# A two-layer hybrid decoder trunk on one Trainium2 core: FFN, norms, gate stages, indexer, attention and output moved from the compiler framework's order into the kernel's own list scheduler

## The chip, the core and the metric

The kernel runs on one core of one Trainium2 chip. A core has five engines, each with an instruction queue of its own that is worked off in the order in which the program has it: PE (TensorE, matrix products and transposes by product with the identity, results in PSUM), DVE (VectorE), ACT (ScalarE), POOL (GpSimd) and SP (SyncE, which here only issues DMAs). The engines wait for each other through semaphores. The metric is the device time of one execution in microseconds; the kernel before has a median of 2846.68 us in 3 runs (2844.36 to 2846.99).

## What is computed

One sequence of 256 tokens, 2048 wide, in f32, through two layers. Cut to what matters:

```python
for i in range(2):
    h = gdn_mixer(x, ...) if i == 0 else dsa_mixer(x, ...)
    x = layer_norm(ALPHA * x + h, ln1_g[i], ln1_b[i])
    f = (silu(causal_conv3(x @ w_gate[i])) * (x @ w_up[i])) @ w_down[i]   # 2048 -> 5120 -> 2048
    x = layer_norm(ALPHA * x + f, ln2_g[i], ln2_b[i])
    x = x + sigmoid(x @ ple_w_gate[i]) * (p[i] @ ple_w_proj[i])
```

`gdn_mixer` is gated DeltaNet linear attention: a projection to 12,352 columns, a causal convolution over four tokens on q, k and v, 32 value heads, the delta rule in chunks, an output norm gated by silu(z) and a projection from 4096 back to 2048. `dsa_mixer` is sparse attention: a projection to 5264 columns (2048 q, 512 k, 512 v, 2048 for 16 indexer heads, 128 indexer keys and 16 weights), a layer norm on the indexer keys, a score for each pair of tokens (ReLU products summed over the heads), the 64 best keys of each token, a softmax over those with a bias by distance, and a projection from 2048 to 2048.

## The kernel before

**Products.** An f32 number is held as two halves, hi (rounded to the type that PE multiplies at full rate) and lo (the rest), and a product is hi·hi + lo·hi + hi·lo. Weights come from HBM in blocks of 128x1024 f32 (512 KB; 1024 columns of SBUF are four k-tiles of 256 columns or two of 512): SP issues the load into one of three `raw` buffers, ACT makes hi (`hi`, L205), DVE makes lo (`lo`, L206), three buffers each, and PE works the block off. There are two forms. `gemm_t_steps` (L211) has the weights as the stationary operand and gives transposed results, `mm_ps`, two PSUM tiles of 128 columns of weights each: per k-tile two products of 512 columns with hi (L224: both halves of x at once) and two of 256 with lo (L228). `gemm_steps` (L236) has x stationary, `b_ps`, two tiles for the two halves of 128 tokens: per k-tile and half L248, L249 (x hi and x lo with the weights' hi) and L252 (with their lo). PSUM has four `mm` tiles, two `sp` and two `bk`. `xT` is x transposed in hi and lo, `x` the residual stream, two tiles of 128 tokens.

**Two ways of ordering.** The DeltaNet part (`gdn_plan`, L413 on) is already placed by the kernel's own list scheduler, `Plan` (L70 to L158). Every piece of work is a task with an engine, an estimated cost, the tasks that it follows, the buffers that it takes and gives, and a rank. `Plan.run` keeps a clock for each engine, and again and again takes the task that can start first, at equal start the one of lowest rank, and emits its instructions; the order in which an engine's tasks are emitted is the order of its queue. The choice is one line (`s` is the estimated start, `at` the engine's clock):

```python
key = (s if s > at + 0.05 else 0.0, rank, t.order)
```

 `place` in it makes five tasks of a weight block: the load (SP, 0.38 us, landing 2.2 us of bus time and 1.8 us later), the cast (ACT 1.06 us, or DVE 0.8), the subtraction (DVE 1.23) and two product tasks (`product(0)` with hi, `product(1)` with lo). The cast and the subtraction have rank 0 when the block is the next one on PE, and 3 otherwise. Everything behind it is written as ordinary code in program order, `project`, `layer_norm`, `ffn`, `prepare`, `ple`, `distances` and `dsa` (L354 to L403 and L1164 to L1410), which the framework schedules with hand-set priorities: weight casts are moved ahead by 1000 places (`W_AHEAD`), the norm is given high priority, and a few orders are forced one by one (`after`).

**What follows the DeltaNet part.** `project` (L1164) multiplies a matrix in five column blocks, adds it to the residual (L324, L326) with its statistics (L328), and then calls `layer_norm`:

```python
blocks = ((0, 512), (512, 512), (1024, 512), (1536, 256), (1792, 256))
```

Before the norm it puts two columns of `ple_w_proj` (`fill`, L1246, into `pw`) on PE as work that doesn't depend on it. `layer_norm` (L354) gets 1/sqrt by an integer guess and three Newton steps (`rsqrt`, L338 to L352), scales tokens 0 to 127 on DVE (L372) and the others on ACT (L373), transposes on PE (`n_ps`, L383), evicts with gain and bias on ACT (`xb`, L389), and makes hi and lo of `xT` on DVE (L392, L393). `affine` (L395) later applies gain (`lng`) and bias (`lnb`) to x itself on DVE (L399, L400), a quarter of the columns at a time, from rows that POOL loads into one buffer each. `ffn` (L1186): 20 column pairs, gate then up, each 256 columns; the convolution and silu of gate and the product with up on ACT and DVE into `hT`; then `project` with `ffn_w_down`, 40 k-tiles. `ple` (L1256): four columns of `ple_w_gate`, the first two side by side, then sigmoid (L1264), times `pw` (L1265), plus x (L1266) and, in layer 0, the transposes of the next x (`t_ps`, L295, with L288 and L289), in layer 1 the store (L1268). `dsa` (L1307): the columns of indexer keys (144 wide) beside the first two indexer heads; the key norm reads its sums out of PSUM (L1319 to L1324); the indexer heads with their small products (L1338); eight loads of the distance bias by POOL (`bias<-fx`, L1356); the 64 best by eight rounds of maximum and replacement; 32 additions of the mask on POOL; keys, values, and then `attend` for each head.

## Time and profile before

| | |
|---|---|
| median of 3 runs | 2846.68 us |
| the profiled execution | 2843.02 us |
| its span, first to last instruction | 2841.2 us |
| weights and other data moved | 519.70 MB, mean 183 GB/s |
| DeltaNet part, to the first norm | about 0 to 893 us |
| FFN of layer 0, to its second norm | about 900 to 1577 us |
| gate stage of layer 0 | about 1580 to 1681 us |
| sparse attention and its projection | about 1677 to 2060 us |
| FFN of layer 1 | about 2065 to 2740 us |
| gate stage of layer 1 and end | about 2742 to 2841 us |

How to read the lines. A row of a group has source line, engine, operation, what it writes <- reads, shape and count, then its busy time and the mean of one, then the idle time of that engine ahead of it and what ended it. In a row of the timeline the first number is the start in us from the span's start, the second the time from the first start to the last end, `x8` a run of eight, and in brackets the engine's idle time ahead of it and what ended that. Matmuls are pipelined, so their busy times overlap; what one costs in a stream is the step from start to start. In a row of a stretch stand its length, then each engine's busy time and instruction count, the granted share of PE's clock, the DMA engines' busy share and GB/s.

### The profile page before, as it was taken

What the parts mean: (1) busy time and instruction counts of PE and PEld (TensorE: products, weight loads), DVE (VectorE), ACT (ScalarE), POOL (GpSimd) and SP (SyncE); (2) the same over time, 40 slices, a digit from 0 to 9 for tenths busy, and PEclk for the clock granted to TensorE, in tenths of its full rate; (3) what the DMA queues carried; (4) which work ended last, traced back from release to release, by engine and by line L of the source; (5) the groups of instructions that cost most, each with busy time, mean ns of one, the idle gap of its engine ahead of it and who ended that gap; (6) DMA issues with size and microseconds to landing.
All of it is one profiled execution on the core that took longest, in us unless ns stands there. A gap on an engine that the chain in (4) does not pass through costs nothing. (4 is left out here: it accounts for less than half of the span.)

```text
span 2841.2 us, 40908 instructions
## 1 busy us (share of the span) xinstructions
PE 2806.2 (99%) x15654; PEld 2436.4 (86%) x15654; DVE 1900.9 (67%) x2995; ACT 1397.7 (49%) x2244; POOL 114.6 (4%) x191
## 2 busy tenths in 40 slices
PE   8999999999999999999999999999999999999998
PEld 7888888888888888888889788888888888888887
DVE  6887778877778666666544755765676666655465
ACT  4745555553435555555433544455465555543353
POOL 0100001000000000000000000400000000000000
PEclk9999999999999999999999999999999999999999
DMA  6765656555545666666555565544556666655555
GB/s 191 222 184 160 184 151 185 172 153 169 154 134 174 188 202 205 205 202 200 192 193 187 190 197 170 177 147 151 177 183 195 196 190 194 197 191 193 190 188 182
DMA packets 415077, 519.70 MB, mean 183 GB/s; under 512 B 19708, under 2 KB 313984, under 8 KB 414880
## 3 DMA queue, kind: packets, MB, share of 16 engines
q1 hardware_dynamic: 407136, 496.76, 56.6%
q0 software_dynamic: 7744, 20.32, 3.0%
q8 instruction: 123, 2.02, 0.3%
q14 instruction: 74, 0.61, 0.1%
HBM read 512.76 MB, written 7.39 MB: 183 GB/s over the span
## 5 line engine op out<-in xcount | busy, mean ns | idle before, releaser
L206 DVE TENSOR_TENSOR lo<-raw,hi 128x1024 fp32r<-128x1024 f32 (+1 forms) x676 | 827.2, 1225 | 625.5 <-ACT hi L205 616.2
L205 ACT ACTIVATE hi<-raw 128x1024 fp32r<-128x1024 f32 (+1 forms) x676 | 714.1, 1057 | 931.5 <-PE b_ps L249 404.2
L224 PE MATMUL mm_ps<-xT,hi 128*128 128x512 f32 x3136 | 792.1, 394 | 2.8 <-DVE rs L345 1.6
L224 PEld LDWEIGHTS mm_ps<-xT,hi 128*128 128x128 f32 x3136 | 565.1, 189 | 103.6 <-issue 2.6
L228 PEld LDWEIGHTS mm_ps<-xT,lo 128*128 128x128 f32 x3136 | 431.0, 191 | 30.4
L228 PE MATMUL mm_ps<-xT,lo 128*128 128x256 f32 x3136 | 447.4, 284 | 0.0
L539 DVE TENSOR_TENSOR lo<-raw,hi 128x1024 fp32r<-128x1024 f32 x249 | 304.0, 1221 | 48.3 <-ACT hi L531 26.0
L531 ACT ACTIVATE hi<-raw 128x1024 fp32r<-128x1024 f32 x183 | 193.3, 1057 | 192.6 <-PE b_ps L506 84.4
L498 PE MATMUL mm_ps<-xT,hi 128*128 128x512 f32 (+1 forms) x1040 | 264.1, 396 | 4.4 <-ACT hi L531 2.7
L498 PEld LDWEIGHTS mm_ps<-xT,hi 128*128 128x128 f32 (+1 forms) x1040 | 189.5, 189 | 42.9 <-ACT hi L531 3.1
L248 PE MATMUL b_ps<-hi,hTA 128*128 128x512 f32 (+1 forms) x640 | 212.6, 347 | 0.0
L249 PE MATMUL b_ps<-hi,hTA 128*128 128x512 f32 (+1 forms) x640 | 212.4, 347 | 0.0
L248 PE MATMUL b_ps<-hi,xT 128*128 128x512 f32 (+2 forms) x480 | 173.3, 370 | 1.6 <-ACT sg L1264 1.6
L249 PE MATMUL b_ps<-hi,xT 128*128 128x512 f32 (+2 forms) x480 | 173.7, 371 | 0.0
L495 PE MATMUL mm_ps<-xT,lo 128*128 128x256 f32 (+1 forms) x1040 | 149.6, 287 | 0.0
L495 PEld LDWEIGHTS mm_ps<-xT,lo 128*128 128x128 f32 (+1 forms) x1040 | 137.1, 189 | 5.8
L252 PE MATMUL b_ps<-lo,hTA 128*128 128x512 f32 (+1 forms) x640 | 138.6, 347 | 0.0
L248 PEld LDWEIGHTS b_ps<-hi,hTA 128*128 128x128 f32 x640 | 121.3, 190 | 15.0
L249 PEld LDWEIGHTS b_ps<-hi,hTA 128*128 128x128 f32 x640 | 121.4, 190 | 14.9
L252 PE MATMUL b_ps<-lo,xT 128*128 128x512 f32 (+2 forms) x480 | 118.5, 370 | 2.8 <-DVE lo L206 2.8
L252 PEld LDWEIGHTS b_ps<-lo,hTA 128*128 128x128 f32 x640 | 105.2, 190 | 15.0
L248 PEld LDWEIGHTS b_ps<-hi,xT 128*128 128x128 f32 x480 | 90.6, 189 | 17.6 <-ACT sg L1264 2.9
(300 smaller groups left out, 3352.8 us busy)
## 6 DMA issues: line engine op xcount, KB each, us to landing
raw<-in_gdn_w_in SPq DMA_DIRECT2D x193, 512.0 KB, 4.0
raw<-in_ffn_w_gate SPq DMA_DIRECT2D x160, 512.0 KB, 3.9
raw<-in_ffn_w_up SPq DMA_DIRECT2D x160, 512.0 KB, 3.7
raw<-in_ffn_w_down SPq DMA_DIRECT2D x160, 512.0 KB, 3.6
raw<-in_dsa_w_in SPq DMA_DIRECT2D x80, 512.0 KB, 3.6
raw<-in_gdn_w_o SPq DMA_DIRECT2D x64, 512.0 KB, 3.7
raw<-in_ple_w_gate SPq DMA_DIRECT2D x64, 512.0 KB, 3.9
raw<-in_dsa_w_o SPq DMA_DIRECT2D x32, 512.0 KB, 3.9
```

What stands on the lines that cost most here:

```text
L205: nc.scalar.activation(hi, raw, AF.Copy)
L206: ins = nc.vector.tensor_tensor(lo, raw, hi.bitcast(F32), op=ALU.subtract)
L224: nc.tensor.matmul(q[:m, :], hi[:, k, o:o + m], x[:, k0 + k].rearrange("p a b -> p (a b)"), start=k0 + k == 0, stop=False)
L228: nc.tensor.matmul(q[:m, S:], lo[:, k, o:o + m], x[:, k0 + k, 0, :], start=False, stop=k0 + k == kt - 1)
L248: nc.tensor.matmul(ps[a][:, :n], xh, hi[:, k, :], start=k0 + k == 0, stop=False)
L249: nc.tensor.matmul(ps[a][:, :n], xl, hi[:, k, :], start=False, stop=False)
L252: self.last = nc.tensor.matmul(ps[a][:, :n], x(k0 + k)[:, 0, a * P:(a + 1) * P], lo[:, k, :], start=False, stop=k0 + k == kt - 1)
L495: nc.tensor.matmul(ps[o][:m, S:], lo[:, k, o * P:o * P + m], x(k0 + k)[:, 0], start=False, stop=e)
L498: nc.tensor.matmul(ps[o][:m], hi[:, k, o * P:o * P + m], x(k0 + k).rearrange("p a b -> p (a b)"), start=s, stop=False)
L531: nc.scalar.activation(hi, box["raw"], AF.Copy)
L539: nc.vector.tensor_tensor(lo, box["raw"], box["hi"].bitcast(F32), op=ALU.subtract)
```

## The change

`gdn`, `project`, `layer_norm`, `ffn`, `prepare`, `ple`, `distances`, `dsa` and their helpers are gone; the same computation is written as tasks of one `Plan` that covers the whole kernel, from the first load to the last store. In the plan:

- The three stages after DeltaNet open their SBUF areas by a POOL task without instructions (`stage`) that follows all tasks added before it; only what writes into the new area follows it.
- Weight blocks stay in one list, `order`; a block's load now follows the load of the block before (`behind`: emitted after it, without waiting for its end). A block that isn't the next one has rank 3.45 for its cast and subtraction instead of 3.
- `project` has four columns of 512 instead of three and two of 256. The last block of the fourth is cut by token half (`split`): all products of tokens 0 to 127, then those of 128 to 255, each with its own task, so that sum and statistics of the first half follow that half alone. `ple`'s last column is cut in the same way.
- The Newton iteration is one cubic step and one quadratic step instead of three quadratic ones: ten DVE instructions instead of twelve.
- `norm`: residual, statistics, root and scaling have ranks below zero; each eviction may go to ACT or to DVE, the rounding to DVE or to ACT, whichever is free first by the plan's clock; the fills' products, the transposes and the first FFN blocks are tasks of PE that start when their inputs are there by that clock. The first FFN block needs the first two pairs of k-tiles complete.
- `affine`: each load of gain or bias follows a given weight block (in FFN one quarter every 32 blocks; for the gate stage block 16 from the end of what is placed then), its use has rank 4.6, below almost everything.
- `dsa`: ACT copies the indexer keys' sums out of PSUM before the key norm; each bias load follows the product of a later weight block (every third one); small products are tasks with rank 1, ahead of the weight blocks' 5 and 4.
- In the DeltaNet part the tasks stay; some ranks change (table `RANK`), above all for taps, decays and table switches.

The core of the diff:

```diff
+    def add(self, engine, cost, emit, after=(), take=(), give=(), rank=5, lag=None, tail=0.0, bus=0.0, table=None,
+            other=None, behind=()):
...
+        for late, tasks in ((True, after), (False, behind)):
+            for d in tasks:
+                t.left += 1
+                d.then.append((t, late))
...
-            d = add(Q, 0.38, load, take=["raw"], rank=i, bus=2.2, tail=1.8)
-            h = add(A, 1.06, high, [d], take=["hi"], rank=urgent,
-                    other=(V, 0.8, cast, lambda: 3 if i <= plan.now + 1 else 9))
-            l = add(V, 1.23, low, [h], take=["lo"], give=["raw"], rank=urgent)
...
+            near = lambda: i <= plan.now + R["near"]
+            urgent = lambda: 0 if near() else R["later"]
...
+            d = b["load"] = add(Q, 0.38, load, take=["raw"], rank=i, bus=2.2 * size, tail=1.8,
+                                behind=[last["load"]] if i else ())
+            h = add(A, 0.2 + 0.86 * size, high, [d], take=["hi"], rank=urgent,
+                    other=(V, 0.1 + 0.6 * size, cast, lambda: R["cast"] if near() else 9))
+            l = add(V, 0.1 + 1.13 * size, low, [h], take=["lo"], give=["raw"], rank=urgent)
...
+            one, two = (2, 3) if b["halves"] else (0, 1)
...
-                nc.vector.tensor_scalar(zz, zz, -0.5, None, op0=ALU.mult)
...
+            def cubic():
+                y, u, zz = box["y"], box["t"], z()
                 nc.vector.tensor_tensor(u, y, y, op=ALU.mult)
                 nc.vector.tensor_tensor(u, u, zz, op=ALU.mult)
+                nc.vector.scalar_tensor_tensor(u, u, -1.25 / c, u, op0=ALU.add, op1=ALU.mult)
+                nc.vector.scalar_tensor_tensor(y, u, 1.875, y, op0=ALU.add, op1=ALU.mult)
...
-            for _ in range(3):
-                d = add(V, 0.55, step, [d], rank=rank)
+            d = add(V, 0.72, cubic, [d], rank=rank)
+            d = add(V, 0.55, step, [d], rank=rank)
...
+        def project(src, kt, x, ready, scale, opened):
...
+            for nb in range(4):
+                def done(state, task, nb=nb):
+                    for a in range(2):
+                        xs_ = self.x[:, a, nb * 512:(nb + 1) * 512]
+                        d = add(V, 0.69, lambda a=a, xs_=xs_: self.residual(xs_, state["ps"][a], scale),
+                                [task[a] if nb == 3 else task], give=["mm"], rank=-2 if nb == 3 else 1)
+                        stat[a].append(add(V, 0.69, lambda a=a, xs_=xs_: nc.vector.bn_stats(st()[:, a, nb], xs_),
+                                           [d, opened], rank=-2 if nb == 3 else 3))
+                r.append(column(src, 0, nb * 512, 512, kt, x, False, ready, done, split=nb == 3))
...
+            for k0 in range(0, KT, 2):
+                n = 2 if k0 < 4 else 0 if k0 % 4 else 4
+                rank = k0 / 8 - 1
...
+                x = add(E, 0.45, turn, before, take=[tag], rank=1, lag=0.25)
+                turned.append(x)
+                for k in range(2):
+                    x = add(A, 0.565, lambda k=k, f=put_a: f(k), [x, gbd], take=["xb"] * (not k), give=[tag] * k, rank=rank,
+                            other=(V, 0.42, lambda k=k, f=put_v: f(k), lambda rank=rank: rank + R["put"]))
...
+                d = add(G, 0.55, lambda r=r, src=src: nc.gpsimd.dma_start(
+                    out=r(), in_=bass.AP(tensor=src.tensor, offset=src.offset + nb * 512, ap=[[0, P], [1, 512]])),
+                    gate, take=[tag], bus=1.1, tail=3.0)
...
+                    c = add(A, 0.4, lambda a=a, kv=kv: nc.scalar.activation(kv(), state["ps"][a][:, :P + 16], AF.Copy),
+                            [task, opened], give=["mm"], rank=1)
...
+            loads = fetch([order[i0 + 3 * j]["task"] for j in range(8)])
...
+                run(c[3])
...
+                run(w["fill"](0))
+                run(w["fill"](1))
+                pairs, turned = norm(st, stat, gb1)
+                gate, up, down = ffn(w, pairs, ready)
+                run(two(gate(0), up(0)))
+                for n in range(2, D_FF // P, 2):
+                    run(gate(n))
+                    run(up(n))
```

More of the change, by code (lines that the diff above doesn't have):

```diff
@@ L153, in run @@
                 self.room[name].sort()
-            for n in t.then:
+            for n, late in t.then:
                 n.left -= 1
-                n.ready = max(n.ready, t.end + (n.lag if n.engine != t.engine or t.tail else 0.0))
+                if late:
+                    n.ready = max(n.ready, t.end + (n.lag if n.engine != t.engine or t.tail else 0.0))
                 if not n.left:
                     self.enter(n)
-        assert len(self.log) == self.count, (len(self.log), self.count)
+        assert len(self.log) == len(self.tasks), (len(self.log), len(self.tasks))
 class Trunk:
+    RANK = {'near': 1,
+            'later': 3.45,
+            'cast': 3,
+            'soon': 2.5,
+            'due': 2,
+            'tap': 4.5,
+            'rows': 3.5,
+            'solve0': 2.2,
+            'solve1': 3.7,
+            'weigh0': 1.5,
+            'weigh1': 5,
+            'dim': 3,
+            'calm': 1.5,
+            'wild': 4,
+            'swap': 2,
+            'put': 0,
+            'round': 2}
     def __init__(self, nc, tc, ctx, t):
-        self.nc, self.tc, self.t, self.heads = nc, tc, t, {}
+        self.nc, self.tc, self.t = nc, tc, t
         pool = lambda **k: ctx.enter_context(tc.tile_pool(**k))
@@ L321, in residual, with run @@
-    def residual(self, xb, ps, st, scale=ALPHA):
+    def run(self, out):
+        engines = {getattr(mybir.EngineType, e) for e in ("PE", "DVE", "Activation", "Pool", "SP")}
+        with self.tc.manual_schedule(engines=engines):
+            self.build(out)
+    def residual(self, xb, ps, scale):
         if scale == 1.0:
@@ L475, in gdn_plan, with column @@
         order = []
-        def column(src, rows, c0, n, kt, x, wide, ready, done):
+        def column(src, rows, c0, n, kt, x, wide, ready, done, nk=None, split=False):
             state = {}
-            nk = min(1024 // n, kt)
-            first = True
+            nk = nk or min(1024 // n, kt)
+            unit = 0.2274 if n == 512 else max(0.112, n / 2400 + 0.0133)
             out = []
@@ L805, in decays @@
         def decays(g, tile, take, out, back, after=()):
[L807 to L808 removed]
+            d = add(Q, 0.4, lambda: rows_into(g, tile()), [rows["go"], *after], take=[take], rank=lambda: plan.now + R["rows"], bus=2.2, tail=3.5)
+            calm = lambda: R["calm"] if plan.table == "exp" else R["wild"]
             def clamp(a, hs):
@@ new lines, in marked, with soon, folded, fold @@
+        def marked():
+            i = len(order) - 1
+            order[i]["bends"] = True
+            due = []
+            def soon():
+                if not due:
+                    due.append(next((j for j in range(i + 1, len(order)) if "bends" in order[j]), i + 99))
+                return R["soon"] if due[0] <= plan.now + R["due"] else R["tap"]
+            return soon
+        def folded(state, n, task, out, rank=1, take=(), more=()):
+            box = {}
+            def fold():
+                box["t"] = new("fold", [S], 2)
+                nc.scalar.activation(box["t"], state["ps"][n][:, S:], AF.Copy)
+            x = add(A, 0.37, fold, [task, *more], take=["fold"], rank=rank)
+            return add(V, 0.42, lambda: nc.vector.tensor_tensor(out(), state["ps"][n][:, :S], box["t"], op=ALU.add),
+                       [x], take=take, give=["mm", "fold"], rank=rank)
```

975 lines of the change are left out of this document (502 added, 473 removed).

## The prediction

> **What bounds the kernel now.** I read the page's busy times first, then who waits for whom on PE, then the timelines of the places named there.
>
> ```profile
> span 2841.2 us, 40908 instructions
> PE 2806.2 (99%) x15654; PEld 2436.4 (86%) x15654; DVE 1900.9 (67%) x2995; ACT 1397.7 (49%) x2244; POOL 114.6 (4%) x191
> L206 DVE TENSOR_TENSOR lo<-raw,hi 128x1024 fp32r<-128x1024 f32 (+1 forms) x676 | 827.2, 1225 | 625.5 <-ACT hi L205 616.2
> L205 ACT ACTIVATE hi<-raw 128x1024 fp32r<-128x1024 f32 (+1 forms) x676 | 714.1, 1057 | 931.5 <-PE b_ps L249 404.2
> ```
>
> PE is the bound; DVE and ACT have a third and a half of the span free. An order can therefore only win what PE loses by standing, and the casts of 676 weight blocks outside the DeltaNet part, which is planned already, are the work that could newly hold PE up. The list of PE's waits says how much stands:
>
> ```profile
> PE n_ps L383 <- ACT xb L389: 5.8, 8, 0.9
> PE b_ps L252 <- DVE lo L206: 2.8, 2, 1.4
> PE mm_ps L498 <- ACT hi L531: 2.7, 1, 2.7
> PE t_ps L295 <- DVE x L1266: 2.0, 2, 1.6
> PE mm_ps L224 <- DVE rs L345: 1.6, 1, 1.6
> PE b_ps L248 <- ACT sg L1264: 1.6, 3, 0.8
> PE mm_ps L224 <- ACT hi L205: 0.9, 1, 0.9
> ```
>
> The columns are the total, the times and the longest. L498 is the planned part; the other six rows, 14.7 us, stand at the norms (L383), in the gate stages (L252, L295, L248) and where the sparse attention begins (L224). So the ceiling of a mere reordering is about 15 us and what surrounds each stop. FFN gate, up and down have no row at all. A steady stretch there shows why: 575 matmuls, half of them 230 ns apart, half 120 ns, are 100.6 us in 100 us, while DVE is at 65%.
>
> ```profile
> 1100.00:1200.00 100.00, 100.00 (x575) 88.14 (x574) 65.02 (x95) 51.71 (x80) 2.31 (x5) 1.00 0.68 205
> 1098.13 2.00 PE L224 MATMUL mm_ps<-xT,hi 128*128 128x512 f32 x8
> 1099.97 1.12 PE L228 MATMUL mm_ps<-xT,lo 128*128 128x256 f32 x8
> 1100.92 2.00 PE L224 MATMUL mm_ps<-xT,hi 128*128 128x512 f32 x8
> ```
>
> (1098.13 to 1099.97 is 8 steps of 230 ns, to 1100.92 another 8 of 119; a block of 512 KB of weights lasts 2.79 us.)
>
> **The change part by part. Wider last columns.** Each projection ended in two columns 256 wide; now it is one of 512. Both kinds of block carry 512 KB; only their starts matter:
>
> ```profile
> 2704.68 0.28 PE L248 MATMUL b_ps<-hi,hTA 128*128 128x256 f32 x1
> 2707.56 0.28 PE L248 MATMUL b_ps<-hi,hTA 128*128 128x256 f32 x1
> 1605.48 0.39 PE L248 MATMUL b_ps<-hi,xT 128*128 128x512 f32 x1
> 1608.20 0.39 PE L248 MATMUL b_ps<-hi,xT 128*128 128x512 f32 x1
> ```
>
> 2.88 us a block against 2.72. With 4, 40, 16 and 40 k-tiles, four to a block and two columns, there are 50 such blocks: 50 x 0.16 = **8.0 us less**, pure PE work and the surest term.
>
> **Norms.** PE has 24 transposes to do between the last product of the fills and the first gate product:
>
> ```profile
> 893.56 0.65 PE L383 MATMUL n_ps<-ident,x 128*128 128x128 f32 x2
> 896.27 0.33 PE L383 MATMUL n_ps<-ident,x 128*128 128x128 f32 x1 [0.77 <-ACT xb L389]
> 900.36 0.78 PE L224 MATMUL mm_ps<-xT,hi 128*128 128x512 f32 x1
> 896.59 1.22 DVE L206 TENSOR_TENSOR lo<-raw,hi 128x1024 fp32r<-128x1024 f32 x1
> 898.66 1.22 DVE L206 TENSOR_TENSOR lo<-raw,hi 128x1024 fp32r<-128x1024 f32 x1
> 895.21 1.92 ACT L389 ACTIVATE xb<-n_ps,gb 128x256 f32<-128x256 f32 x4
> 892.24 0.16 DVE L351 SCALAR_TENSOR_TENSOR rs<-rt,rs 128x2 f32<-128x2 f32 x1
> ```
>
> Two weight casts of 1.22 us stand between the pieces of xT that PE waits for, and ACT alone evicts four halves in 1.92 us. In the plan the norm's tasks rank ahead of casts that aren't due, and an eviction may go to DVE. The inverse square root takes ten instructions instead of twelve (0.16 us each, row L351), and the statistics of the first 128 tokens run beside the last products of the other 128. Against that, the last sum and statistics are 512 wide, not 256: an estimate of 0.6 us more on the path, half of 0.65 us for each of the two, from the 512-wide DVE rows at the end of the kernel below. The row n_ps has 5.8 us for four norms; DVE must still do scale, round and subtract for two pairs before the first block, so I recover 4.0 of 5.8 (bounds 0 and 5.8).
>
> **Gate stages.**
>
> ```profile
> 1614.57 1.29 DVE L400 TENSOR_TENSOR x<-x,lnb 128x512 f32<-128x512 f32 x2 [3.35 <-DMA lnb<-in_ln_b]
> 1617.05 1.20 PE L252 MATMUL b_ps<-lo,xT 128*128 128x512 f32 x4 [1.44 <-DVE lo L206]
> 1628.06 1.28 ACT L1264 ACT_TABLE_LOAD   x1
> 1629.36 0.60 ACT L1264 ACTIVATE sg<-b_ps 128x512 f32<-128x512 f32 x1
> 1630.01 0.50 PE L248 MATMUL b_ps<-hi,xT 128*128 128x512 f32 x1 [0.85 <-ACT sg L1264]
> 1619.93 1.07 PE L252 MATMUL b_ps<-lo,xT 128*128 128x512 f32 x4
> lnb<-in_ln_b POOLq DMA_DIRECT2D x16, 256.0 KB, 5.8
> ```
>
> DVE waits in its order for the norm's gain and bias rows, the casts stand behind it, PE stands. The plan asks for these rows 16 blocks earlier and puts their use at a low rank; the transposes (the t_ps row, 1.6 at its longest) become tasks that PE takes when they are ready, while it runs the attention's first blocks. Of 2.8 + 2.0 + 1.6 = 6.4 us I recover 5.5 (bounds 3 and 6.4). What speaks against it: the plan reckons 0.55 + 3.0 us for such a load where the row shows 5.8, so DVE can still stand 2 us with casts behind it; three raw, hi and lo buffers, two blocks or 5.4 us, cover that, and without cover it would be 2 us at each of the 8 places.
> The third column needs the sums that the sigmoid frees; from the end of column one it has 2.72 us, and table load and two sigmoids are 1.28 + 1.2 = 2.5, just enough. The Trainium skill (ScalarE: Activation LUTs, What ACT_TABLE_LOAD costs) gives a switch 2.66 us with the drain; by that the column would stand some 1.2 us longer in each stage and the sum be about 2.5 us smaller. Here the sigmoid starts 20 ns after the 1.28 us load, so I keep the row.
>
> **Where sparse attention begins.**
>
> ```profile
> 1682.50 5.95 POOL L1356 DMA_DIRECT2D bias<-fx  x8
> 1690.00:1695.00 5.00, 5.00 (x40) 4.75 (x38) 0.76 (x1) 0.69 (x1) 0.00 (x0) 1.00 1.04 350
> 1705.05 0.70 PE L224 MATMUL mm_ps<-xT,hi 128*128 128x512 f32 x2 [1.58 <-DVE rs L345]
> 1708.15 1.91 PE L228 MATMUL mm_ps<-xT,lo 128*128 128x256 f32 x8
> ```
>
> Eight bias loads go out at once and fill the DMA engines (share 1.04), so weights come late (the 0.9 us row); after it PE waits 1.6 us for the sums that the key norm reads, and then runs at half rate: 1.91 us for the eight steps that took 1.12. The change gates each bias load on a later block, and ACT copies the keys out at once (two copies, each narrower than the 512-wide ACT row of 0.60 us above). The waits added are POOL's: behind each gated load stand only the next one and the mask additions, needed when the heads come. I recover 0.9 + 1.6 + 0.8 = 3.3 (bounds 1 and 3.7).
>
> **Restarts and end.** A stop costs more than its idle time: the four products at 1617.05 take 1.20 us instead of the 1.07 of the group at 1619.93; the six rows count 17 stops, and 15 fewer at 0.13 are 2.0 (bounds 0.5 and 2.5).
>
> ```profile
> 2834.92 1.09 ACT L1264 ACTIVATE sg<-b_ps 128x512 f32<-128x512 f32 x2 [7.78 <-PE b_ps L252]
> 2836.76 1.29 DVE L1266 TENSOR_TENSOR x<-x,sg 128x512 f32<-128x512 f32 x2
> ```
>
> At the end two halves go through sigmoid, product and sum together, 3.1 us. With the last block cut by halves the first is done under the second's products; one half needs 2.0: **1.0 less** (0.3 to 1.2).
>
> **What it costs.** FFN, which loses nothing, now depends on estimated times. In the planned part the one cast row is L498, 2.7 us, at the very start. I charge 2.5 us (bounds 0 and 9, the latter 13 ns for each of 676 blocks). The new ranks inside the DeltaNet part I put at 0 (2 either way): PE's rows there are mostly the start.
>
> **Sum.** 8.0 + 4.0 + 5.5 + 3.3 + 2.0 + 1.0 - 2.5 = **21.3 us**. The profiled execution took 2843.0 us, its span and 1.8 us around it; it would take 2821.7. The median of the runs is 2846.68, 3.7 us above that execution; the predicted median is 2846.7 - 21.3 = **2825.4**. Lower bounds alone give 8 + 0 + 3 + 1 + 0.5 + 0.3 - 9 = 3.8, or 2843; the upper ones with 2 us from DeltaNet 8 + 5.8 + 6.4 + 3.7 + 2.5 + 1.2 + 2 = 29.6, or 2817.
>
> **Rivals.** *Casts come late* (slower). The plan makes a cast urgent only when its block is next. Cast and subtraction are 1.06 + 1.23 = 2.3 us against a block's 2.79; half a microsecond of fold or tap ahead of them in a fixed order and PE stands. Its size is the 0.9 us of the L224 row; in one block of fifteen that is 676 / 15 x 0.9 = 41 us, against gains of 23.8: 2864. It decides from one block in 26 (35 ns a block). For it: three buffers only. Against it: DVE at 65% in the FFN, and a single such row in the planned part. 8%.
> *The stops only move* (no change; also the case in which the plan's clock is so far from the chip's that its order isn't what it takes it for). The named waits go, but equal ones arise at the same joints, since DVE is the limit there; only the wide columns and the end remain, less the FFN's charge at its worst: 8 + 1 - 9 + 2 = 2, up to 8: 2839 to 2845. For it: at the first norm DVE is busy 12.16 us of 12.58. 18%.
>
> ```profile
> 887.78:900.36 12.58, 10.64 (x52) 8.36 (x50) 12.16 (x34) 9.80 (x17) 0.00 (x0) 0.89 0.32 94
> ```
>
> *Half rate at every joint.* That row's clock, 0.89, shows a stretch at half rate after PE's idling. If all four norms and the gate stages met such a stretch, each would cost up to twice the 0.8 us seen above, some 5 us in all: 2830. The Trainium skill (TensorE: Matmul & The Clock Gate, the part on the HAM clock gate) halves the clock after one idle window of 3.4 us that runs freely; which joint is hit is then chance. The row agrees that it happens. 5%.
> *More than that*: the plan also fills the remaining stops; 2810 to 2815. 7%.
>
> **How the numbers follow.** The forecast, 2815 to 2837, has 62%. From 2813 to 2843 lies that, the clock case and most of the second rival: about 80%. Under 0.2% (5.7 us) this kernel's measurement can't tell a change from none. Faster than 2841.0: 62 + 5 + 7 and 8 of the second rival's 18, 82%; within it the other 10%; slower 8%.
>
> **What would show it.** Right: no L206-like row over 1 us among PE's waits, n_ps under 2 us, no 128x256 products in the projections, DMA share under 0.9 where attention begins, the last store about 1 us nearer to the last product. Wrong: PE rows on hi or lo spread over many times in FFN (first rival), or n_ps, t_ps and sg rows of the old size under new lines (second).

## The result and the profile after

The changed kernel takes **2816.85 us** (median of 4 runs, 2816.54 to 2818.76) against 2846.64 for the kernel before (4 runs beside it, 2844.36 to 2846.99): ratio 0.9898, 95% interval 0.9881 to 0.9916, 1.0% less time. The prediction had 2825.4 with a range of 2813 to 2843.

The profiled execution took 2816.92 us. It is 26.1 us shorter than the profiled execution of before, the medians differ by 29.8, since that execution of before lay 3.6 us under its median. Over all 42 runs of the kernel before in this document the median is 2843.3 us, and against that the gain is 26.4 us; some 3 us of the 29.8 belong to the four runs that happened to stand beside the changed kernel. The head of its page:

```profile
span 2815.1 us, 39629 instructions
PE 2789.1 (99%) x15054; PEld 2402.5 (85%) x15054; DVE 1889.9 (67%) x2932; ACT 1416.1 (50%) x2259; POOL 115.2 (4%) x191
```

PE has 600 matmuls fewer (the narrow columns' second halves) and stays the bound. Where the 26.1 us came from is read by cutting both traces at the same pieces of work (start to start of the first product of each kind):

| stretch | before, us | after, us | difference |
|---|---|---|---|
| start to first product | 5.28 | 5.13 | -0.2 |
| to the last product of the DeltaNet output | 882.50 | 882.23 | -0.3 |
| to the first down product, layer 0 (norm 1, FFN) | 461.75 | 459.93 | -1.8 |
| to norm 2 (down) | 226.86 | 224.70 | -2.2 |
| to the indexer keys (norm 2, gate stage) | 101.01 | 96.44 | -4.6 |
| to norm 3 (sparse attention and its projection) | 381.48 | 366.72 | **-14.8** |
| to the first down product, layer 1 (norm 3, FFN) | 453.37 | 455.09 | **+1.7** |
| to norm 4 (down) | 226.86 | 224.68 | -2.2 |
| to the last product (norm 4, gate stage) | 95.62 | 94.67 | -1.0 |
| end | 6.53 | 5.57 | -1.0 |

More than half of it is the sparse attention, to whose start the prediction gave 3.3 us. The stretch with norm 3, which was to gain, lost.

**Who waits for whom on PE, after.** Columns: the total, the times, the longest.

```profile
PE mm_ps L303 <- DVE xT L1116: 2.9, 2, 2.0
PE b_ps L310 <- DVE xT L1113: 2.6, 2, 1.3
PE n_ps L1089 <- ACT x L1081: 2.3, 5, 0.6
PE b_ps L310 <- DVE hi L345: 1.8, 2, 1.2
PE b_ps L311 <- DVE oT L934: 1.1, 1, 1.1
```

(The rows for `hi` and `oT` stand in the DeltaNet part; the list's other rows stand in the kernel's first 100 us or have 0.5 us at most.) The rows of the gate stages (lo, sg, t_ps) and of the start of the attention (rs) are gone. At the norms n_ps fell from 5.8 to 2.3, but 2.9 + 2.6 us of waits for `xT` are new: the stop moved from the transposes to the first product behind them.

**Norm 3 after**, timeline: start, time from first start to last end, engine, line, what it writes <- reads.

```profile
2034.20 3.49 DVE L349 TENSOR_TENSOR lo<-raw,hi 128x1024 fp32r<-128x1024 f32 x3
2034.41 1.06 ACT L341 ACTIVATE hi<-raw 128x1024 fp32r<-128x1024 f32 x1 [0.77 <-PE b_ps L311]
2035.38 1.08 ACT L1081 ACTIVATE x<-x,lnm,rs 128x256 f32<-128x256 f32 x2
2036.02 1.04 PE L1089 MATMUL n_ps<-ident,x 128*128 128x128 f32 x7 [0.60 <-ACT x L1081]
2036.36 0.58 ACT L1038 ACTIVATE pw<-b_ps 128x512 f32<-128x512 f32 x1
2036.84 1.91 ACT L1100 ACTIVATE xb<-n_ps,gb 128x256 f32<-128x256 f32 x4
2039.08 3.58 PE L303 MATMUL mm_ps<-xT,hi 128*128 128x512 f32 x8 [2.03 <-DVE xT L1116]
```

In this trace a cast (1.06) stands on ACT ahead of the scaling, a `pw` copy ahead of the evictions, three subtractions (3.49) on DVE, and all four evictions are ACT's. Then the first eight products take 3.58 us, where eight take 2.0 elsewhere. The stretches around them (length, each engine's busy time, PE's granted clock, DMA share, GB/s) say why:

```profile
2035.49:2038.90 3.41, 1.04 (x7) 0.73 (x7) 3.19 (x4) 3.41 (x8) 0.00 (x0) 1.00 0.59 179
2038.90:2042.32 3.42, 3.24 (x8) 2.56 (x9) 1.62 (x4) 1.04 (x2) 0.00 (x0) 0.50 0.87 282
```

In the second stretch the clock is halved for 3.41 us. This document calls such a stretch a half-rate window. Before has three ahead of its last product (norms 1 and 2, start of the attention), after has two (norms 3 and 4).

**The body of the attention.** PE's list of waits for before names one stop of 0.2 us there. The list for PE's weight loads (PEld, the instructions that bring a product's stationary operand into PE) does:

```profile
PEld po_ps L1404 <- ACT prT L1401: 4.2, 15, 0.4
PEld sc_ps L1338 <- PE mm_ps L224: 1.8, 6, 0.5
PEld tp_ps L1399 <- issue: 1.7, 7, 0.3
PEld lg_ps L1388 <- DVE qq L285: 1.4, 7, 0.2
```

9.1 us in 35 short stops, none over 0.5 us; after has no row for these four. One place, before:

```profile
1890.59 0.47 ACT L1401 ACTIVATE prT<-tp_ps 128x384 f32<-128x384 f32 x1
1890.65 0.40 PE L224 MATMUL mm_ps<-xT,hi 128*128 128x512 f32 x1
1891.11 0.30 PEld L1404 LDWEIGHTS po_ps<-prT,vv 128*128 128x128 f32 x2 [0.39 <-ACT prT L1401]
1891.12 0.49 PE L1404 MATMUL po_ps<-prT,vv 128*128 128x128 f32 x2
1891.81 1.64 PE L224 MATMUL mm_ps<-xT,hi 128*128 128x512 f32 x6
```

A product that streams in 0.23 us starts at 1890.65, the next only at 1891.12: the mixed values (`po`) stand in the midst of a weight block, and their operand leaves ACT at 1891.06. The product's own modelled end (0.40) covers nearly the whole stop, so PE counts as busy. After, the same groups stand between the halves of blocks, joined for two heads, and their inputs are there in time (`pr` 0.9 us, `prT` 0.2 us before the groups that read them):

```profile
1874.78 2.01 PE L303 MATMUL mm_ps<-xT,hi 128*128 128x512 f32 x8
1876.62 0.82 PE L1451 MATMUL tp_ps<-ident,pr 128*128 128x128 f32 x6
1877.19 1.20 PE L300 MATMUL mm_ps<-xT,lo 128*128 128x256 f32 x8
1878.23 0.38 PE L1459 MATMUL po_ps<-prT,vv 128*128 128x128 f32 x2
```

1874.78 to 1876.62 are eight undisturbed steps of 230 ns. Counted over the whole stage from start to start, against the undisturbed step of each shape, before loses 8.8 us in 87 steps on entering these groups and within them, after 0.15 us in two.

**The end, after**, the second half of the tokens:

```profile
2809.58 0.39 PE L313 MATMUL b_ps<-lo,xT 128*128 128x512 f32 x1
2810.01 0.60 ACT L1251 ACTIVATE xb<-b_ps 128x512 f32<-128x512 f32 x1 [0.76 <-PE b_ps L313]
2811.36 0.69 DVE L1255 TENSOR_TENSOR x<-x,xb 128x512 f32<-128x512 f32 x1
```

From the last product 2.5 us to the last sum, as against 3.3 before.

### The profile page after: what moved, and what is told of

Read it like the earlier page. It is cut to its first block, busy times and chain, and to the rows that moved or that the text cites. A ratio compares the mean times of both kernels' runs of the same rounds, so it can differ in the third digit from the quotient of the medians.

```text
span 2815.1 us, 39629 instructions
## 1 busy us (share of the span) xinstructions
PE 2789.1 (99%) x15054; PEld 2402.5 (85%) x15054; DVE 1889.9 (67%) x2932; ACT 1416.1 (50%) x2259; POOL 115.2 (4%) x191
## 4 chain that ended last, share of the span: by engine, by line
PE 68%; DVE 1%; DMA 0%; ACT 0%; issue 0%; ACTq 0%
PE mm_ps L303 26%; PE mm_ps L300 13%; PE b_ps L311 9%; PE b_ps L310 9%; PE b_ps L313 9%; DMA raw<-in_dsa_w_in 0%; PE lg_ps L1425 0%; PE sc_ps L1339 0%; PE n_ps L1089 0%; PE tp_ps L1451 0%; PE po_ps L1460 0%; PE po_ps L1461 0%; PE po_ps L1459 0%; PE t_ps L1266 0%; DVE lo L349 0%
## 5 line engine op out<-in xcount | busy, mean ns | idle before, releaser
L349 DVE TENSOR_TENSOR lo<-raw,hi 128x1024 fp32r<-128x1024 f32 x925 | 1130.1, 1224 | 708.2 <-ACT hi L341 684.0
L341 ACT ACTIVATE hi<-raw 128x1024 fp32r<-128x1024 f32 x877 | 926.6, 1057 | 1105.5 <-PE mm_ps L303 481.8
L303 PE MATMUL mm_ps<-xT,hi 128*128 128x512 f32 (+1 forms) x4176 | 1053.4, 394 | 7.6 <-ACT hi L341 3.9
L303 PEld LDWEIGHTS mm_ps<-xT,hi 128*128 128x128 f32 (+1 forms) x4176 | 754.2, 189 | 149.0 <-ACT hi L341 4.9
L300 PEld LDWEIGHTS mm_ps<-xT,lo 128*128 128x128 f32 (+1 forms) x4176 | 564.1, 190 | 35.7 <-issue 0.2
L300 PE MATMUL mm_ps<-xT,lo 128*128 128x256 f32 (+1 forms) x4176 | 589.7, 284 | 0.0
L310 PE MATMUL b_ps<-hi,xT 128*128 128x512 f32 (+1 forms) x704 | 272.2, 389 | 4.4 <-DVE xT L1113 2.6
L311 PE MATMUL b_ps<-hi,xT 128*128 128x512 f32 (+1 forms) x704 | 270.7, 387 | 0.2 <-DVE xT L1116 0.2
L310 PE MATMUL b_ps<-hi,hTA 128*128 128x512 f32 x512 | 199.2, 389 | 0.0
L311 PE MATMUL b_ps<-hi,hTA 128*128 128x512 f32 x512 | 199.2, 389 | 0.0
L313 PE MATMUL b_ps<-lo,xT 128*128 128x512 f32 (+1 forms) x704 | 188.3, 388 | 0.0
L311 PEld LDWEIGHTS b_ps<-hi,xT 128*128 128x128 f32 x704 | 133.0, 189 | 26.4 <-DVE xT L1116 1.0
L311 PE MATMUL b_ps<-hi,oT 128*128 128x512 f32 x256 | 100.3, 392 | 1.1 <-DVE oT L934 1.1
L310 PE MATMUL b_ps<-hi,oT 128*128 128x512 f32 x256 | 100.6, 393 | 0.0
```

Source lines behind the costliest of these rows:

```text
L300: nc.tensor.matmul(ps[o][:m, S:], lo[:, k, o * P:o * P + m], x(k0 + k)[:, 0], start=False, stop=e)
L303: nc.tensor.matmul(ps[o][:m], hi[:, k, o * P:o * P + m], x(k0 + k).rearrange("p a b -> p (a b)"), start=s, stop=False)
L310: nc.tensor.matmul(ps[o][:, :n], xh, hi[:, k, :], start=s, stop=False)
L311: nc.tensor.matmul(ps[o][:, :n], xl, hi[:, k, :], start=False, stop=False)
L313: nc.tensor.matmul(ps[o][:, :n], xh, lo[:, k, :], start=False, stop=e)
L341: nc.scalar.activation(hi, box["raw"], AF.Copy)
```

## The experiments

All are timed in alternation with the kernel before, whose 42 runs lie between 2839.55 and 2846.99 us; its median was 2846.64 beside the changed kernel and 2843.92, 2842.55 and 2841.66 in the three later rounds. A difference of one or two us between the medians of two versions is therefore not read by itself, and the stretches of the traces are compared besides. The down stretches, and what lies from the last transpose of norm 3 to the first down product, repeat to 0.02 us where an edit leaves them alone (436.82 or 436.83 in six traces). The DeltaNet stretch doesn't: in eight traces of plan kernels whose edit leaves it alone it takes 880.9 to 882.8; the attention takes 366.3 to 367.1 in six. Half-rate windows ahead of the last product, from the granted clock of each trace, are given with each run; the changed kernel has two. What the theories were at the start: that the gain of the attention comes from where the small groups stand (rival: from the wider columns, the bias loads or the key norm), and that the norms gained nothing because the plan lets weight work in ahead of them (rival: the norm's own chain is the stop).

**1. Columns narrow again.** `project` of the changed kernel:

```diff
-            for nb in range(4):
+            for nb, (c0, n) in enumerate(((0, 512), (512, 512), (1024, 512), (1536, 256), (1792, 256))):
```

> The changed kernel with one part undone: the four projections end in two columns 256 wide again. If the columns' term is what the prediction made of it, 50 blocks at 2.88 instead of 2.72 us, this takes 8.0 us (6 to 9) more than the changed kernel's 2816.9. If the blocks' length was only the look of two isolated blocks, the difference is under 3 us.

2821.86 us (2821.28 to 2822.65), 5.0 more; two windows. The two down stretches are 2.54 and 2.57 us longer, the attention's 0.8, 5.9 together; the stretches with the norms sum to -0.3, with two windows on each side, and the DeltaNet stretch is 1.4 shorter, as much as it scatters. So undoing the columns here costs 6 us, not 8; 0.6 of what each down stretch lacks is the slow steps of one tile, which only 512-wide products show in full (last section).

**2. Columns wide, alone, in the kernel before.**

```diff
-        blocks = ((0, 512), (512, 512), (1024, 512), (1536, 256), (1792, 256))
+        blocks = ((0, 512), (512, 512), (1024, 512), (1536, 512))
-        for _ in range(kt // 4 - 1):
+        for _ in range(kt // 2 - 1):
```

> The kernel before with one part of the change alone: the projections' last columns 512 wide. The columns' term by itself: 8.0 us less than the kernel before (6 to 9), thus about 2838 to 2840. If the norms that follow lose what the wider last sum and statistics cost, 0.6 us each, it is 5.6 us less.

2846.08 us (2839.64 to 2848.03, 11 runs) against 2843.92: no gain, ratio 1.0006 (0.9997 to 1.0015). Yet the down stretches are 223.67 and 223.69 instead of 226.86 and the attention's projection is 1.3 shorter: 7.7 us of products did go, as the term has it. But this trace has **eight** half-rate windows instead of three. One of the new ones, behind a stop in the gate stage:

```profile
1616.37:1619.79 3.42, 1.54 (x7) 0.99 (x6) 2.72 (x4) 2.12 (x2) 0.00 (x0) 1.00 0.35 131
1619.79:1623.20 3.41, 3.41 (x9) 2.65 (x9) 1.98 (x2) 0.00 (x0) 0.00 (x0) 0.50 0.65 201
```

At half rate a window loses at most half of 3.41 us, 1.7, so five more lose up to 8.5 us, about the whole gain. That is a reckoning: the stretches with norms 2, 3 and 4, which hold four of the five, are 8.6 us longer together, more than four windows can lose, so part of it is longer stops. Neither number of the expectation came.

**3. Clock alone.** Ten transposes of the identity ahead of the first product behind norms 2, 3 and 4, into sums that this product starts anew:

```diff
+                        for _ in range(warm):
+                            nc.tensor.transpose(state["ps"][0][:, :P], self.ident, self.ident)
```

> The changed kernel with ten transposes of the identity added ahead of the first product of the gate columns behind norms 2, 3 and 4; they write sums that the first product then starts anew, so they only give PE work in its stops of 1.5 to 2.2 us there (ten steps of 0.11 are 1.1 us). Theory, from the windows of the runs so far: a clock window of 3.41 us in which PE worked less than about 1.6 us is followed by a window at half rate, and each of those costs 1.7 us. Then the two half-rate windows behind norms 3 and 4 go and nothing else moves: 3.4 us less than the changed kernel, granted clock 1.000. Rival: the half rate follows from the stop as such (no weight product in it), not from how little PE works; then the windows stay and the time is the same or up to 1 us longer.

2813.45 us (2812.90 to 2813.73), 3.4 less; no window. The stretches with norms 3 and 4 are each 1.3 us shorter, that with norm 2, which had no window, is the same; the rest of the 3.4 lies in the DeltaNet stretch and the attention, which scatter by as much. At norm 3 PE does useless work in its stop, and the clock stays up:

```profile
2035.96 1.25 PE L294 MATMUL mm_ps<-ident 128*128 128x128 f32 x10
2038.15 2.03 PE L305 MATMUL mm_ps<-xT,hi 128*128 128x512 f32 x7 [0.94 <-DVE xT L1118]
```

Seven products follow in 2.03 us (seven at 0.23 are 1.6, and the last one's end), where after needs 3.58 for eight. The theory holds as to the cause, and the rival falls; the price of a window is 1.3 us here, not 1.7. The same shows at norm 2: in the five kernels of experiments 6, 8, 9, 10 and 12, which have a window there that the changed kernel hasn't, that stretch is 1.1 to 1.6 us longer.

**4. Norm first.** The first casts, subtractions and the last `pw` copies held behind the norm's own scaling, evictions and roundings (`behind` orders without a wait):

```diff
+        def hold(blocks, n, pairs, evicted, scaled):
+
+            blocks[0]["late"] = (), [scaled[1][0]]
+            for b in blocks[1:3]:
+                b["late"] = [evicted[n]], [pairs[n][1]]
+            return blocks
```

> The changed kernel with the casts and subtractions of the first blocks behind a norm, and the second half of the copies of the fills, held behind the norm's own evictions and roundings. Theory: the norms gained nothing because the plan's clock lets weight work in ahead of the norm's on ACT and DVE (three subtractions of 1.2 us behind the scaling of norm 3, a cast and a copy between its two scalings). Then PE's standing at the four norms falls by 0.7 to 1.5 us each and the two windows at half rate behind norms 3 and 4 (1.7 us each) go: 3 to 6 us less than the changed kernel. Rival: the chain of scale, transpose, evict, round, subtract is itself the length of the stop, whoever stands beside it; then the difference is under 1.5 us, or it is positive because the casts come late for the first blocks.

**2809.38 us** (2809.28 to 2811.04), 7.5 less than the changed kernel; ratio to before 0.9882 (0.9869 to 0.9896). No window. The stretches with norms 1 to 4 give 0.8, 0.8, 2.7 and 2.0 us, 6.3 in all. Two windows in them are gone, 2.6 by experiment 3, so the order itself gives some 3.7; the rest lies in the DeltaNet stretch, which scatters by as much. Norm 3 in it:

```profile
2030.75 0.73 DVE L1081 TENSOR_SCALAR x<-x,lmv,rs 128x256 f32<-128x256 f32 x2
2030.87 1.10 ACT L1083 ACTIVATE x<-x,lnm,rs 128x256 f32<-128x256 f32 x2 [0.27 <-DVE lnm L1072]
2032.34 1.14 PE L1091 MATMUL n_ps<-ident,x 128*128 128x128 f32 x9
2032.98 1.02 ACT L1102 ACTIVATE xb<-n_ps,gb 128x256 f32<-128x256 f32 x2 [1.01 <-PE n_ps L1091]
2033.89 0.81 ACT L1083 ACTIVATE x<-x,lnm,rs 128x512 f32<-128x512 f32 x1
2034.75 0.98 PE L1091 MATMUL n_ps<-ident,x 128*128 128x128 f32 x7 [1.26 <-ACT x L1083]
```

ACT scales beside DVE, and nine transposes run at once. 1.26 us stay, for the next scaling behind two evictions. This is the fastest version here.

**5. The same, and the second tokens' scaling may go to DVE.**

```diff
+                            other=(V, 0.14 + 0.13 * n, lambda x1=x1: nc.vector.tensor_scalar(
+                                x1, x1, mv()[:, 1, 0:1], r()[:, 1:2], op0=ALU.subtract, op1=ALU.mult),
+                                lambda rank=rank: rank))]
```

> The version with the norm ahead of weight work, and beside it the second tokens' scaling may go to DVE where DVE is free sooner. Theory: the stops of 1.4 us that remain at the norms are waits for ACT's scaling of the second pieces behind its own evictions, so 1 to 4 us less than that version (which took 2809.4). Rival: DVE is the tighter engine there (its weight subtractions come later), so no gain or up to 3 us more.

2822.19 us (2820.04 to 2823.80): 12.8 more than version 4; two windows. The whole order behind each norm came out anew, and the largest of the new PE waits are for the `pw` copies that free PSUM:

```profile
PE b_ps L310 <- ACT pw L1039: 5.0, 2, 2.6
PE n_ps L1094 <- DVE x L1081: 3.3, 3, 1.1
PE mm_ps L303 <- ACT pw L1039: 2.1, 1, 2.1
PE mm_ps L300 <- DVE lo L349: 2.1, 1, 2.1
```

Worse by far more than the rival allowed. The rival named DVE, and two of the four rows, 5.4 of 12.5 us, are DVE's; the others are ACT's. The expectation looked at one chain; the plan re-placed several.

**6. Evictions by ACT alone.** The alternatives `other=(V, 0.42, ...)` and `other=(A, 0.62, ...)` taken out of `norm`.

> The changed kernel with one part undone: the norm's evictions go to ACT alone and its roundings to DVE alone. By the prediction, which counted on evictions by DVE, the four norms lose some 0.5 to 1 us each, 2 to 4 us. By the trace of the changed kernel, where ACT did the first four evictions of norm 3 anyway, the difference is within 1 us.

2818.13 us (2816.34 to 2819.64); three windows. The stretches with the four norms are 1.7 us longer together, of which 1.5 is the one with norm 2, where the third window stands. The choice of engine, on which the prediction's norm term leaned, was worth nothing that these traces show.

**7. No cut by token halves.**

```diff
-                r.append(column(src, 0, nb * 512, 512, kt, x, False, ready, done, split=nb == 3))
+                r.append(column(src, 0, nb * 512, 512, kt, x, False, ready, done))
```

> The changed kernel with the last column of each projection and of each gate stage no longer cut by token halves. The prediction's term for the end says that the last store then comes 1.0 us (0.3 to 1.2) later after the last product; its remark on the norms, that the statistics of the first half run under the products of the other, adds up to 0.6 us at each of the four norms, so 1 to 3.5 us in all. If the cut does nothing at the norms (they gained nothing in the trace), it is the 1.0 us of the end alone.

2817.84 us (2814.56 to 2819.25); three windows. From the last product to the end 6.67 us instead of 5.57: **1.1 us**, the end's term. The stretches with norms 2 and 3 are each 0.4 us shorter without the halving, that with norm 4 is the same, and that with norm 1 is 1.8 longer, with the third window in it: the halving gains nothing at the norms.

**8. Bias loads behind one early block.**

```diff
-            loads = fetch([order[i0 + 3 * j]["task"] for j in range(8)])
+            loads = fetch([order[i0 - 7]["task"]] * 8)
```

> The changed kernel with one part undone: the eight bias loads of the sparse attention go out together again, behind one early block. The prediction gave the burst 0.9 us (a late cast) and a part of what lies around it; so 0.5 to 2 us more than the changed kernel. If the bias loads are a large part of the 14.8 us that this stage gained, the difference is 4 us or more.

2824.82 us (2823.34 to 2825.57), 8.0 more; five windows, two of them at the start of the attention, whose stage is 6.0 longer. It is not the DMA burst. The eight loads go out in a burst in the changed kernel too, where each was to follow a block of its own:

```profile
L1363 POOL DMA_DIRECT2D bias<-fx x8: 747/748/764, 1670.9 to 1676.1; - x8
```

(count, duration, first and last start) and the stretch behind it:

```profile
1680.00:1685.00 5.00, 5.00 (x39) 4.65 (x38) 0.76 (x1) 0.68 (x1) 0.00 (x0) 1.00 1.05 347
```

The loads start within 5.2 us, with a DMA share of 1.05 behind them; in the kernel before it is 5.2 and 1.04. The blocks that they follow in the plan belong to the second and later pairs of indexer heads and run behind 1688 us, when the keys' columns have ended; the loads had gone by then. They share no data with these blocks, so "follows" set their place in the plan's clock and made no wait on the chip. With the edit they start at the same place, 2.5 us behind the keys' first product. What the edit changed is the plan's order: both transposes of the keys and the first scores now stand together, ahead of weight blocks that they followed, and PE waits for the key norm's chain of DVE instructions, with two half-rate windows behind it:

```profile
PE ki_ps L1320 <- DVE ki L1314: 3.7, 2, 2.7
```

**9. Key norm reads PSUM itself.** ACT's copies taken out, `give=["mm"]` put on the key norm's scaling.

> The changed kernel with one part undone: the key norm reads the sums in PSUM itself, without ACT's copy, and holds them until its own scaling. The prediction gave the wait for these sums 1.6 us and the half rate behind it 0.8: so 1.5 to 2.5 us more. If the plan gets round it by taking other sums, under 0.7 us.

2824.18 us (2822.45 to 2825.45), 7.3 more; five windows. The stage is 6.3 longer: PE stands twice, and the two windows behind it are at half rate.

```profile
1694.69 0.30 PE L1317 MATMUL ki_ps<-ident,ki 128*128 128x128 f32 x1 [2.54 <-DVE ki L1311]
1694.81 0.69 PE L303 MATMUL mm_ps<-xT,hi 128*128 128x512 f32 x1
1697.38 2.05 PE L303 MATMUL mm_ps<-xT,hi 128*128 128x512 f32 x4 [1.87 <-DVE ki L1310]
```

The direction was foreseen, the size was about three times it.

**10. Small groups planned earlier.** `lag=-0.4` instead of 0.6 at the three task lines of `attend`.

> The changed kernel in which PE's small groups of the sparse attention (logits, turned probabilities, mixed values) are planned 1 us earlier after their inputs than in the change, so that some stand in PE's order before what they read is there. Theory: the 14.8 us that the sparse attention gained, where 3.3 were forecast, come from these small groups no longer standing in the midst of a block before their inputs; undoing a part of that costs 4 to 12 us, and the list of the weight loads' waits shows rows for po, tp and lg again. Rival: the gain comes from another place (the wider columns, the joined groups of small products); then it is under 1.5 us more.

2819.19 us (2818.41 to 2821.20); three windows. The stage takes 366.7 as in the changed kernel; stops on entering small groups are 0.8 us in 14 steps instead of 0.15 in two. The 2.4 us of the medians lie elsewhere: 1.5 in the stretch with norm 2, where the third window stands. By the stage's time the rival would have it. But the groups had moved by half a block and their inputs were mostly still there: the dose was too small to decide.

**11. Small groups later, in the kernel before.** There `attend` and `index` are plain code. Their pieces were put on a list and written out a number of weight blocks later:

```diff
-            tp = self.sp.tile([P, 3, P], F32, tag="bk", name="tp_ps")
+            later.append([2, lambda: turn(h, j, pr)])
+
+        def turn(h, j, pr):
+            tp = self.sp.tile([P, 3, P], F32, tag="bk", name="tp_ps")
...
+        def paced(*args):
+            for _ in self.gemm_t_steps(*args):
+                for e in [e for e in later if e[0] <= 0]:
+                    later.remove(e)
+                    e[1]()
+                for e in later:
+                    e[0] -= 1
```

> The kernel before with one thing changed by hand: in the sparse attention the small groups of a head are written out later: scores one weight block after their column, logits one block after it, turned probabilities two blocks after the logits, mixed values one block after those. Theory: the kernel before loses 8.8 us in 87 short stops on entering these groups and within them, because they stand in PE's order before their inputs; so the stage from the keys to norm 3 becomes 6 to 9 us shorter than the 381.5 of the kernel before. Rival: the gain of that stage comes from the stops at its beginning and the half-rate window there alone (4.6 and 2.1 us); then the stage gains under 2 us.

2834.56 us (2829.89 to 2838.51, 10 runs), 7.1 less than the kernel before; ratio 0.9973 (0.9964 to 0.9982). The stage is 373.6 instead of 381.5, **7.9 us** less; the stops on entering small groups fell from 8.8 us in 87 steps to 0.8 in ten, while the stage still has its three long stops (4.4 for 4.6) and one half-rate window. In PEld's list each of the four rows, 9.1 us before, is down to one stop of 0.2. So the small groups alone are worth 7 to 8 us here, shown by adding this one thing to the old kernel.

**12. The old ranks.** The table `RANK` of before in the changed kernel.

> The changed kernel with one part undone: the plan's table of ranks as it was before, which bears on the DeltaNet part above all. The prediction put the new ranks at 0 us, 2 either way. From the first product to the last block of the DeltaNet output the kernel before took 882.5 us and the changed one 882.2; a difference of more than 2 us in this stretch would make the term wrong.

2823.37 us (2821.92 to 2824.93); three windows. The DeltaNet stretch takes 885.3 instead of 882.2, 3.1 us more, all of it two stops:

```profile
PE v_ps L792 <- DVE oT L920: 2.8, 2, 1.6
```

That is outside the 2 us of the term and outside the scatter of this stretch (880.9 to 882.8), so inside the plan the new ranks do save 2.5 us or more. Between the kernel before and the changed one the stretch moved by only 0.3; what gave the saving back is not shown. The changed kernel has a stop of 1.1 us at its last head (`oT`, in the list above) which the list for the kernel before hasn't.

## Why the prediction was right or wrong

The direction was right, the time lies in the range, and the mechanism holds as far as it goes: stops of PE at the joints went, and no cast after the DeltaNet part came late by more than 0.3 us. But that the sum came so near is partly luck: the norms gave 3.7 us less than forecast, a place that no term named gave 7.3, and some 3 us of the difference of the medians belong to the four runs of before. By the prediction's own steps, against the traces:

| term | predicted | traces |
|---|---|---|
| wider last columns | 8.0 | 8.0 in the products |
| norms | 4.0 | 0.3, with two half-rate windows before and after |
| gate stages | 5.5 | 7.1 |
| start of sparse attention | 3.3 | 4.3 |
| restarts | 2.0 | 0.7; otherwise contained in the rows above |
| end | 1.0 | 1.0 |
| FFN | -2.5 | -2.7, for another reason |
| DeltaNet, start | 0 | 0.1 |
| small groups of the attention | not seen | 7.3 |
| sum | 21.3 | 26.1 |

(The traces' column: columns are 3.2 us in each down stretch and 1.3 in the attention's projection, as experiment 2 has them, and 0.3 for the DeltaNet output's two blocks by the prediction's 0.16 a block; gate stages the stops of before at 1615 to 1631 us, 3.1, at 2776 to 2790, 2.2, and at 1678, 1.8; norms what is then left of their four stretches; start of the attention the stops from the keys' columns to the first score, 5.6 before without the one at 1678, half rate included, and 1.3 after; restarts a small transpose with two slow steps, 0.36 us, that stands in each down stretch of before alone; small groups what is then left of the attention's 14.8.)

- **The step that failed** is the first one: "So the ceiling of a mere reordering is about 15 us and what surrounds each stop", read from PE's list of waits. That list doesn't hold a stop that the modelled end of the matmul ahead of it covers (0.40 us for a step of 0.23 at 1890.65). 9.1 us of such stops stood in the list for PE's weight loads, and the steps from start to start in the attention, read as they were for the FFN, show them. Experiment 11 takes them out of the old kernel and gets 7.9 us.
- **Norms** (4.0, bounds 0 and 5.8): 0.3, at the lower bound. The prediction took the ranks at their word: "In the plan the norm's tasks rank ahead of casts that aren't due". By the line of code that chooses, a rank decides only between tasks that can start at the same time by the plan's clock; a cast that can start before the scaling goes first, as it does at norm 3 above. The rival "the stops only move" (18%) came true here, and here alone. Experiment 4 forces the order and gets some 3.7 us at the four norms beside the windows; so the 4.0 was there, and the change didn't collect it. "An eviction may go to DVE" is worth nothing (experiment 6), nor are "the statistics of the first 128 tokens" beside the last products (experiment 7).
- **Gate stages**: right, and over the upper bound of 6.4, since stops were taken by their waits and not from start to start. The third column, which had "just enough" time for table load and sigmoid, shows no wait. The Trainium skill's 2.66 us for a switch (ScalarE: Activation LUTs, What ACT_TABLE_LOAD costs) would, by the prediction's estimate, have left a stop of some 1.2 us in each stage. The trace doesn't agree: no row of after has such a stop, and in both stages the sigmoid starts within 0.02 us of the end of a load of 1.28 us, as before.
- **Start of the attention**: "The change gates each bias load on a later block" is true of the plan and not of the chip; the loads go out in 5.2 us as before, and the DMA share named as a sign, under 0.9, didn't come (1.05). The stops shrank all the same. The copies of the keys by ACT are part of that (experiment 9 takes them out and loses 6.3 us of the stage); the place that the key norm and its transposes got in the order is another (experiment 8 changes only the order and loses 6.0).
- **Columns**: the surest term is right as work. As time it isn't additive: in the old kernel alone it bought nothing (experiment 2), in a trace with five more half-rate windows.
- **FFN**: "casts come late" did not happen; gate and up have no row, and take the same within 0.1 us. The 2.7 us are 1.3 to 1.4 in each down product, by the steps of one tile (last section); that the charge of 2.5 comes near is luck.
- **The rival "half rate at every joint"** is half right: the change moved the windows from norms 1 and 2 and the attention to norms 3 and 4. Its price was too low: 1.1 to 1.6 us a window (experiment 3), where 0.8 for eight products was taken.
- **The signs**: no `lo` row over 1 us, no narrow columns and a last store 1.0 us nearer came; n_ps under 2 us (it is 2.3) and the DMA share didn't.

What stays open: what gave back inside the DeltaNet stretch what the ranks saved, and how the small groups' share divides between ending their stops and joining them: it is 7.3 us as the rest here, 7.9 in experiment 11 and 8.8 by the old kernel's own count.

## What to carry to other kernels

Look for PE's lost time in steps from start to start, or in the list of its weight loads' waits; its own list of waits hid the 8.8 us of stops that matmuls' modelled ends cover. A list scheduler's rank isn't an order, nor is its "follows" a wait: where one chain must come first, force it (`behind`), and look in the trace at what the plan's clock made of it; an edit of one task can re-place a whole joint. In this kernel a stop of some 2 us cost 1.1 to 1.6 us more where it left a window of the clock mostly empty, so count half-rate windows first when two variants differ by a few us, and shorten or fill the stop that makes them.

## What the runs showed of the hardware

- **Half rate without an idle window.** The granted clock falls to 0.50 for 3.41 us at a time, at places that lie whole multiples of 3.413 us apart within a run and elsewhere in the next run. That grid was laid over all 14 traces with PE's work in each window taken from start to start, each step at most its undisturbed length. From 20 us on, each window that ran at full rate with less than about 1.25 us of work was followed by one at half rate, none with more than about 1.65 was, and in between both occur. The window ahead of norm 3's in after held 0.77 us of work; filled by ten transposes it kept the clock (experiment 3). The Trainium skill (TensorE: Matmul & The Clock Gate, the part on the HAM clock gate) has windows of this length that run freely, which agrees, and half rate after one *idle* window, which is too mild: here a window that is some two thirds empty is enough.
- **Scatter of the old kernel.** Its 42 runs spread over 7.4 us, the four of the version without windows over 1.8 (experiment 4). That windows which fall or don't fall make this scatter is not shown: each kernel has one trace, and the granted clocks of the old kernel's runs don't go with their times (2842.3 us in the mean of 11 runs at 0.997, 2843.4 of 23 at 0.998).
- **One tile's steps.** In the down products of the changed kernel the stationary operand `hTB` gives steps of 234 ns, `hTA` 227; in the kernel before both give 227. At 7 ns more, the 192 products with this tile are the 1.3 to 1.4 us that each down stretch lost. Between 1400 and 1500 us, after, then before:

```profile
L310 PE MATMUL b_ps<-hi,hTA 128*128 128x512 f32 x128 | 49.8, 389 | 0.0
L310 PE MATMUL b_ps<-hi,hTB 128*128 128x512 f32 x19 | 7.5, 396 | 0.0
```

```profile
L249 PE MATMUL b_ps<-hi,hTB 128*128 128x512 f32 x22 | 8.6, 389 | 0.0
```

(Mean of one 396 against 389 ns.) Shape, type and source of the weights are the same; the tile is allocated in another way since the change, so it can lie in another place of SBUF. Whether that is the cause wasn't tried.
